# A hybrid encoder layer on one core: x's first two K tiles first, attention's stores by another queue, the last product in two halves

## The chip, the core and the metric

The kernel runs on one core of a Trainium2 chip. The core has a matrix engine (PE, TensorE), three elementwise engines (DVE, the VectorE; ACT, the ScalarE; POOL, the GpSimd) and a queueing engine (SP, the SyncE) that here only starts DMA transfers. ACT and POOL can start transfers too. Each engine runs its own list of instructions in order and waits on semaphores for the others. The metric is the device time of one execution in microseconds, and the median of the runs is what is compared.

## The reference, cut to what matters

x is 1024 tokens by 2048 features in float32. The layer is

```python
def hybrid_layer(x, w_in, w_out, norm_w, decay_fwd, decay_bwd, gn_w, gn_b, sink):
    h = rms_norm(x, norm_w)
    proj = h @ w_in                    # 2048 -> 6656 columns
    rq, rk, rv, rg, aq, ak, av, ag = jnp.split(proj, splits, axis=-1)
    y_ret = retention_branch(rq, rk, rv, decay_fwd, decay_bwd, gn_w, gn_b) * jax.nn.silu(rg)
    y_att = window_attention_branch(aq, ak, av, sink) * jax.nn.silu(ag)
    y = jnp.concatenate([y_ret, y_att], axis=-1)
    return x + y @ w_out               # 2048 -> 2048
```

and a last RMS norm with final_norm_w follows it. Retention has 8 heads of 128 in chunks of 128 tokens, scanned in both directions. The attention has 8 query heads over 2 key and value heads, with a window of 128 tokens on either side and a rotation of the first 32 dimensions.

## The kernel before

**Matmuls.** Every float32 operand is split into a rounded high part and a low part (`split`: a cast on ACT into the high part, then a subtraction on DVE, L84, into the low part), and a product is three matmuls (`mm3`: L98 high by high, L99 and L100 the mixed ones). A matmul of 128x128 by 128x512 is the unit. A K step of an operand pair is 6 of them, and `advance()` is called after each K step of the projection: this is a **tick**. The input projection runs block by block with seven products in place of eight (`PRODUCTS`, in the order 1, 2, 6, 5, 7, 3, 4). Each product has four K steps, that is 24 matmuls. The operands on the side of x are combined once (`put`), kept in DRAM by `keep`, and read back as `c<-kept` by `reload` in the second pass over x's other half of K (`reload` issues one transfer, then idles three ticks). The first block is computed directly (`first_block`), since x isn't yet normalised: the rows of x are scaled by the norm's weights only, and the factor of each token is put in afterwards.

**The start.** Token rows are tiles of 128. Rows 0 to 3 of x come first, as four transfers of one row tile and four K tiles each (128x512). PE transposes them (L1026) into four banks; ACT rounds (`rounded`, L911) and DVE takes the remainder (`left_over`, L915) of each K tile, and `first_block` can start. The 4 x 4 transposes, and turns of the identity that fill the gaps (`turn_ident`), precede the first matmul. Rows 4 to 7 come later. Their squares are summed (`squares`, L371 on ACT, L373 on DVE), the factor is computed (`factors_of`, with a power on POOL, L382), the rows are scaled (`scale_x`), and `rest_of_x` turns them (`turn_x`, L395) one K tile a tick after 15 ticks, with one `split` each.

**The factor of rows 0 to 3** comes later still (`scale_first`, started from `rest_of_x` at its fourth turn): it is spread along a row by a transpose (L960), and DVE multiplies (L965, 12 instructions of 128x512) the eight tiles of `src0` and the four results of the first block that were held unscaled.

**What runs beside the projection.** Generators (`jobs`) are advanced one step a tick: attention, retention and gating each issue a few instructions per tick. The order on PE, SP and POOL is the order of the program text. On ACT and DVE a scheduler orders the instructions from tick 33 to the last product, apart from those that are pinned; before and after that they have the program's order too. Attention first rotates k and q (`rotate`: load `rx` by SP, wait `idle(5)` ticks, then three DVE instructions, L493 and L91, then store). Then `heads(0)`, `(2)`, `(4)` and `(6)` load two query heads each (`q<-pr`), split them (`qbH`, `qbL`), and store their results into `mix` (L602, on SP's queue), 16 stores of 256 KB. A tile of q is overwritten by the head's result, so the next load of q waits for the stores. Results of the projection are stored by SP (the first time) or by POOL's queue with accumulation (L258, the second time).

**The end.** The output projection ends with the product (p, t) = (3, 3). Its bank is added to the residual (`add`, L91), squared and summed (L1305), and `finish` (L1327 to 1337) multiplies by the factor and the weight and stores two halves of 1024 columns of the last row tile. For row tile 6 the same is done by ACT (L1307), POOL (L1310, L1311) and `finish`.

## Time and profile before

| | us |
|---|---|
| median of 3 runs | 1531.56 |
| lowest and highest of them | 1530.33, 1531.64 |
| the profiled execution | 1533.51 |
| its span in the profile | 1531.70 |

The rows shown below are from one profiled execution. Its own time is 1.81 us above its span and 1.95 us above the median. A row of the timeline gives the start in us from the span's beginning, the duration, the engine and line, output and inputs, and how often the instruction is repeated in the row; in brackets stands how long the engine stood idle before it, and what released it. A matmul's duration is longer than the distance to the next one, because matmuls are pipelined: what a step costs is read from start to start. A name with q (SPq, POOLq) means the queueing side of an engine.

### The profile page before, as it was taken

What the parts mean: (1) busy time and instruction counts of PE and PEld (TensorE: products, weight loads), DVE (VectorE), ACT (ScalarE), POOL (GpSimd) and SP (SyncE); (2) the same over time, 40 slices, a digit from 0 to 9 for tenths busy, and PEclk for the clock granted to TensorE, in tenths of its full rate; (3) what the DMA queues carried; (4) which work ended last, traced back from release to release, by engine and by line L of the source; (5) the groups of instructions that cost most, each with busy time, mean ns of one, the idle gap of its engine ahead of it and who ended that gap; (6) DMA issues with size and microseconds to landing.
All of it is one profiled execution on the core that took longest, in us unless ns stands there. A gap on an engine that the chain in (4) does not pass through costs nothing.

```text
span 1531.7 us, 20492 instructions
## 1 busy us (share of the span) xinstructions
PE 1513.6 (99%) x7414; PEld 1273.8 (83%) x7414; DVE 1084.5 (71%) x1940; ACT 690.3 (45%) x1148; POOL 151.8 (10%) x169
## 2 busy tenths in 40 slices
PE   9999999999999999999999999999999999999997
PEld 7788888788888888887888888888888888888886
DVE  6985594557857585746977797779655966776766
ACT  7643363234535453533444434443444643542425
POOL 0000001111010000011212100001111102020001
PEclk9999999999999999999999999999999999999999
DMA  8268656889674415687677655488689769395756
GB/s 302 83 224 297 245 191 167 213 221 253 153 209 135 138 69 179 233 312 203 129 186 197 189 177 193 151 294 295 181 206 256 156 197 265 87 204 163 221 176 254
DMA packets 150533, 306.59 MB, mean 200 GB/s; under 512 B 13440, under 2 KB 71200, under 8 KB 141472
## 3 DMA queue, kind: packets, MB, share of 16 engines
q1 hardware_dynamic: 125632, 250.74, 48.1%
q0 software_dynamic: 19728, 36.71, 15.4%
q10 hardware_dynamic: 5072, 17.84, 3.4%
q8 instruction: 58, 0.95, 0.3%
q14 instruction: 43, 0.35, 0.1%
HBM read 190.68 MB, written 122.95 MB: 205 GB/s over the span
## 4 chain that ended last, share of the span: by engine, by line
PE 78%; issue 13%; DVE 3%; DMA 3%; ACT 1%; POOL 1%; SPq 0%; POOLq 0%; ACTq 0%; DVEq 0%
PE pj L100 19%; PE pj L99 19%; PE pj L98 19%; PE ax L99 5%; PE ax L100 5%; PE ax L98 5%; PE ax L787 2%; PE ax L509 1%; PE ax L586 1%; DMA xt<-in_x_dram 1%; PE ax L754 1%; PE ax L834 1%; DMA c<-kept 1%; DVE c L84 1%; DMA pr<-ct 1%
## 5 line engine op out<-in xcount | busy, mean ns | idle before, releaser
L98 PE MATMUL pj<-c,wH 128*128 128x512 f32 x1448 | 578.6, 400 | 0.3 <-DVE ct L91 0.3
L99 PE MATMUL pj<-c,wH 128*128 128x512 f32 x1448 | 565.3, 390 | 3.2 <-DMA c<-kept 1.7
L100 PE MATMUL pj<-c,wL 128*128 128x512 f32 x1448 | 566.1, 391 | 1.9 <-DVE wL L84 1.9
L100 PEld LDWEIGHTS pj<-c,wL 128*128 128x128 f32 x1448 | 271.8, 188 | 61.8 <-DVE wL L84 4.0
L99 PEld LDWEIGHTS pj<-c,wH 128*128 128x128 f32 x1448 | 272.5, 188 | 54.9 <-DVE c L84 2.2
L98 PEld LDWEIGHTS pj<-c,wH 128*128 128x128 f32 x1448 | 272.3, 188 | 50.4 <-ACT ct L268 0.6
L87 ACT CAST wH<-a 128x1024 fp32r<-128x1024 f32 (+1 forms) x160 | 167.6, 1048 | 248.0 <-PE pj L99 144.9
L84 DVE TENSOR_TENSOR wL<-a,wH 128x1024 fp32r<-128x1024 f32 (+1 forms) x160 | 194.7, 1217 | 112.2 <-ACT wH L87 108.8
L268 ACT COPY ct<-pj 128x512 f32<-128x512 f32 x200 | 116.1, 585 | 234.9 <-PE pj L100 234.3
L91 DVE TENSOR_TENSOR ct<-pj,ct 128x512 f32<-128x512 f32 x170 | 113.2, 689 | 61.4 <-PE pj L100 60.2
L258 POOL DMA_DIRECT2D pr<-ct x104 | 92.3, 962 | 621.9 <-DVE ct L91 474.6
L84 DVE TENSOR_TENSOR wL<-s,wH 128x1024 fp32r<-128x1024 f32 x56 | 68.5, 1223 | 91.7 <-ACT wH L87 91.6
L99 PE MATMUL pj<-wL,c 128*128 128x512 f32 x224 | 87.2, 390 | 0.2 <-DVE wL L84 0.2
L98 PE MATMUL pj<-wH,c 128*128 128x512 f32 x224 | 87.1, 389 | 0.0
L100 PE MATMUL pj<-wH,c 128*128 128x512 f32 x224 | 87.1, 389 | 0.0
L99 PE MATMUL ax<-wL,c 128*128 128x512 f32 x208 | 81.1, 390 | 0.0
L98 PE MATMUL ax<-wH,c 128*128 128x512 f32 x208 | 80.9, 389 | 0.0
L100 PE MATMUL ax<-wH,c 128*128 128x512 f32 x208 | 80.9, 389 | 0.0
L87 ACT CAST wH<-s 128x1024 fp32r<-128x1024 f32 x56 | 59.1, 1056 | 16.4 <-PE ax L100 8.8
L99 PEld LDWEIGHTS pj<-wL,c 128*128 128x128 f32 x224 | 42.0, 188 | 9.4 <-DVE wL L84 0.7
L87 ACT CAST sH<-st 128x128 fp32r<-128x128 f32 x112 | 29.9, 299 | 44.2 <-DVE st L801 28.2
L98 PEld LDWEIGHTS pj<-wH,c 128*128 128x128 f32 x224 | 42.0, 188 | 8.8
(227 smaller groups left out, 2039.9 us busy)
## 6 DMA issues: line engine op xcount, KB each, us to landing
a<-in_w_in_dram SPq DMA_DIRECT2D x103, 512.0 KB, 5.9
kept<-c SPq DMA_DIRECT2D x28, 1024.0 KB, 7.9
c<-kept SPq DMA_DIRECT2D x28, 1024.0 KB, 10.1
pr<-ct SPq DMA_DIRECT2D x104, 256.0 KB, 4.5
pr<-ct POOLq DMA_DIRECT2D x104, 256.0 KB, 6.3
a<-in_w_out_dram SPq DMA_DIRECT2D x18, 512.0 KB, 5.2
rx<-pr SPq DMA_DIRECT2D x64, 128.0 KB, 3.8
ysrc<-mix ACTq DMA_DIRECT2D x16, 512.0 KB, 5.2
```

Source lines behind the costliest of these rows:

```text
L84: nc.vector.tensor_tensor(out=dst, in0=src, in1=high.bitcast(F32), op=ALU.subtract)
L87: nc.scalar.copy(out=dst_h, in_=src)
L91: nc.vector.tensor_tensor(out=dst, in0=a, in1=b, op=ALU.add)
L98: nc.tensor.matmul(po, aH, bH, start=first, stop=False, **kw)
L99: nc.tensor.matmul(po, aH, bL, start=False, stop=False, **kw)
L100: nc.tensor.matmul(po, aL, bH, start=False, stop=last, **kw)
L258: nc.gpsimd.dma_start(out=dst, in_=t, accum_op=ALU.add)
L268: nc.scalar.copy(out=t, in_=bank)
L509: nc.tensor.transpose(pt[:, blk(t)], src[:, blk(b * 4 + t)], ident)
L586: nc.tensor.transpose(pt[:, blk(j)], s[:, blk(j)], ident)
L754: nc.tensor.matmul(sc[:, blk(t)], kT[:, c], qT[:, c], start=True, stop=True)
L787: nc.tensor.matmul(p, k_tok[:, c], vd[:, c, d], start=True, stop=True)
```

## The change

It has six parts.

1. **Start.** The first transfers of x carry two K tiles of two row tiles each, so that K tiles 0 and 1 of all four row tiles arrive first: SP starts row tiles 0 and 1, ACT row tiles 2 and 3. `first_of_first(0)` transposes and splits these two K tiles; the matmuls of the first tick follow, and only then K tiles 2 and 3 (`first_of_first(1)`). The squares of row tiles 0 to 3 move from the start to ticks 11 to 17. The second half of these rows (`xs[5]`, 2 transfers of 1 MB) is loaded at tick 9. `rest_of_x` begins one tick earlier.
2. **Factors of rows 0 to 3.** `scale_first` is started from `sums_of_x` after its last sum. Of the twelve multiplications, four stay on DVE and eight go to POOL (128x512 each).
3. **Rotation.** The first half of the rotation of k waits 8 ticks in place of 5. `put(5)` keeps its place in the order.
4. **Attention's 16 stores into `mix`** go to POOL's queue.
5. **Reload** idles 2 ticks in place of 3.
6. **Last product.** It is computed in two column halves of 256, each followed by its addition, sum of squares and weighting; the final multiplication and the stores are split 768, 512 and 768 columns.

```diff
 def rotate(pool, table, sets, wait):
...
-                yield from idle(5)
+                yield from idle(wait if m == 0 else 5)
...
-                            nc.sync.dma_start(out=mix[RH + i + h][:, half(n // 4)], in_=q[:, h, half(n // 4)])
+                            nc.gpsimd.dma_start(out=mix[RH + i + h][:, half(n // 4)], in_=q[:, h, half(n // 4)])
...
-            yield from rotate_att(att, (T_AK, T_AK + 1))
+            yield from rotate_att(att, (T_AK, T_AK + 1), wait=8)
...
-    load_x(nc.sync, 0)
+    load_first(nc.sync, 0, 0)
     nc.scalar.dma_start(out=vec, in_=norm_w[0].rearrange("(k p) -> k p", p=P))
     half_of_a11(0)
-    load_x(nc.scalar, 1)
-    load_x(nc.sync, 2)
-    load_x(nc.scalar, 3)
+    load_first(nc.scalar, 2, 0)
+    load_first(nc.sync, 0, 1)
+    load_first(nc.scalar, 2, 1)
     half_of_a11(2)
...
+    def first_of_first(c):
+
+        for t in range(4):
+            for k in (2 * c, 2 * c + 1):
+                nc.tensor.transpose(pts[k][:, blk(t)], xh[t, 0][:, blk(k)], ident)
+        if c == 0:
+            prepare()
+        else:
+            split(*(t[:, 2:4] for t in ops_of_a11), a11[:, 2:4])
+        for k in (2 * c, 2 * c + 1):
+            rounded(0, k, pts[k])
+            left_over(0, k, pts[k])
+        for k in (2 * c, 2 * c + 1):
+            keep_bank(0, k, pts[k])
+
     def rest_of_first():
         yield
+        first_of_first(1)
...
 def scale_first():
 
+        yield
+        yield
         factors, rows = ct(), ct()
...
-        for s in range(2):
-            for k in range(M):
-                scale(src0[:, s, k, half(0)])
-                if k % 2:
-                    yield
+        for k in range(M):
+            scale(nc.vector, src0[:, 0, k, half(0)])
+            scale(nc.gpsimd, src0[:, 1, k, half(0)])
+        yield
         yield from idle(31 - clock[0])
         for first, dst, e in unscaled:
-            scale(e)
+            scale(nc.gpsimd, e)
...
-        yield from idle(15)
+        yield from idle(14)
...
-                put(i)
+                put(i, i == 5)
...
-                yield from idle(3)
+                yield from idle(2 if part == 0 else 3)
...
+    def last_half(c, t, bank, rs):
...
+        add(r[:, at], bank, r[:, at])
+        junk = pools["op"].tile([P, HALF], BF16, name="junk", bufs=1)
+        nc.vector.tensor_tensor_reduce(out=junk[:, at], in0=r[:, at], in1=r[:, at], scale=1.0 / D, scalar=rs[c - 1] if c else part[tt],
+                                       op0=ALU.mult, op1=ALU.add, accum_out=rs[c])
+        if c:
+            nc.gpsimd.tensor_tensor(out=rs[1], in0=rs[1], in1=neg_half[:, 0:1], op=ALU.pow)
+        nc.vector.tensor_tensor(out=row[:, to], in0=r[:, at], in1=fw[:, to], op=ALU.mult)
+        if c:
+            lo, hi = 3 * D // 8, 5 * D // 8
+            nc.vector.tensor_scalar(out=row[:, hi:], in0=row[:, hi:], scalar1=rs[1], scalar2=None, op0=ALU.mult)
+            nc.scalar.mul(row[:, :lo], row[:, :lo], rs[1])
+            nc.sync.dma_start(out=out[blk(tt), hi:], in_=row[:, hi:])
+            nc.vector.tensor_scalar(out=row[:, lo:hi], in0=row[:, lo:hi], scalar1=rs[1], scalar2=None, op0=ALU.mult)
+            nc.scalar.dma_start(out=out[blk(tt), :lo], in_=row[:, :lo])
+            nc.sync.dma_start(out=out[blk(tt), lo:hi], in_=row[:, lo:hi])
...
+                            for kk in range(M):
+                                wH, wL = w[p][kk // 2]
+                                mm3(b[:, cols], c[:, 0, kk, blk(t)], c[:, 1, kk, blk(t)], wH[:, kk % 2, cols], wL[:, kk % 2, cols],
+                                    h == 0 and kk == 0, kk == M - 1, skip_group_check=True)
+                            last_half(h, t, b[:, cols], rs)
```

DVE while rows 4 to 7 are turned and the factors of rows 0 to 3 put in. `c` from `src` is the low part of a turned K tile (512 wide) or of `put` (1024 wide), `src<-src,ct` is the factor's multiplication, `wL` the low part of a weight. Before:

```order
L965 TENSOR_TENSOR src<-src,ct 128x512 x2
L84 TENSOR_TENSOR wL<-a_175,wH 128x1024
L84 TENSOR_TENSOR c_512<-src,c_512 128x512
L965 TENSOR_TENSOR src<-src,ct 128x512 x2
L84 TENSOR_TENSOR c_512<-src,c_512 128x512
L965 TENSOR_TENSOR src<-src,ct 128x512 x2
L84 TENSOR_TENSOR c_205<-src,c_205 128x1024
L965 TENSOR_TENSOR src<-src,ct 128x512 x2
L84 TENSOR_TENSOR c_205<-src,c_205 128x1024
```

The same stretch of DVE now, and after it the rows of POOL that hold the moved multiplications:

```order
L84 TENSOR_TENSOR c_492<-src,c_492 128x512 x2
L84 TENSOR_TENSOR wL<-a_175,wH 128x1024
L84 TENSOR_TENSOR c_492<-src,c_492 128x512
L986 TENSOR_TENSOR src<-src,ct 128x512 x4
L84 TENSOR_TENSOR c_203<-src,c_203 128x1024 x2
L84 TENSOR_TENSOR wL<-a_184,wH 128x1024
L84 TENSOR_TENSOR c_204<-src,c_204 128x1024 x2
```

```order
L377 TENSOR_TENSOR rms<-rms,neg_half 128x2 x2
L377 TENSOR_TENSOR rms<-rms,neg_half 128x4
L986 TENSOR_TENSOR src<-src,ct 128x512 x4
L986 TENSOR_TENSOR ct<-ct 128x512 x4
L252 DMA pr_105<-ct 128x512
L252 DMA pr_106<-ct 128x512
```

The multiplications no longer stand between the subtractions of the turned K tiles; four stand behind them on DVE and eight on POOL ahead of its first store.

DVE at the second half of the rotation of k. `rx` is the piece that is rotated, `ct` the result of a product, `wL` the weight of the next one. Before:

```order
L91 TENSOR_TENSOR ct<-pj,ct 128x512 x2
L84 TENSOR_TENSOR wL<-a_2118,wH 128x1024
L493 TENSOR_TENSOR rx_2369<-rx_2369,rt_2365 64x512
L493 TENSOR_TENSOR rx_2370<-rx_2370,rt_2366 64x512
L91 TENSOR_TENSOR ct<-pj,ct 128x512
L91 TENSOR_TENSOR rx_2369<-rx_2369,rx_2370 64x512
L91 TENSOR_TENSOR ct<-pj,ct 128x512
L84 TENSOR_TENSOR wL<-a_2318,wH 128x1024
```

Now:

```order
L91 TENSOR_TENSOR ct<-pj,ct 128x512 x2
L84 TENSOR_TENSOR wL<-a_2110,wH 128x1024
L91 TENSOR_TENSOR ct<-pj,ct 128x512 x2
L84 TENSOR_TENSOR wL<-a_2310,wH 128x1024
L486 TENSOR_TENSOR rx_2382<-rx_2382,rt_2378 64x512
L486 TENSOR_TENSOR rx_2383<-rx_2383,rt_2379 64x512
L91 TENSOR_TENSOR rx_2382<-rx_2382,rx_2383 64x512
```

The product's two additions and the next weight's low part now precede all three instructions of the rotation.

ACT where `heads(2)` loads its queries. `q<-ax` is the last result of the two heads before, `qbH` the high part of the new queries, `wH` that of a weight. Before:

```order
L599 COPY q<-ax 128x2x2x128
L87 CAST wH<-a_3072 128x1024
L87 CAST wH<-a_3581 128x1024
L87 CAST qbH<-q 128x256 x2
L268 COPY ct<-pj 128x512
```

Now:

```order
L592 COPY q<-ax 128x2x2x128
L87 CAST wH<-a_3064 128x1024
L87 CAST qbH<-q 128x256 x2
L87 CAST wH<-a_3573 128x1024
L262 COPY ct<-pj 128x512
```

The cast of a weight now stands behind the two casts that wait for the queries' load.

## Rows read from the trace of the kernel before

**Rows 1.** Page, part 1: busy us, share of the span and instructions of each engine.

```profile
PE 1513.6 (99%) x7414; PEld 1273.8 (83%) x7414; DVE 1084.5 (71%) x1940; ACT 690.3 (45%) x1148; POOL 151.8 (10%) x169
```

**Rows 2.** Timeline of PE: the first matmuls of the first product.

```profile
10.20 0.50 PE L98 MATMUL pj<-c,wH 128*128 128x512 f32 x1
10.98 0.50 PE L99 MATMUL pj<-c,wH 128*128 128x512 f32 x1 [0.28 <-DVE c L915]
```

**Rows 3.** Windows: length; busy PE, PEld, DVE, ACT, POOL; clock, DMA share, GB/s.

```profile
20.00:30.00 10.00, 9.89 (x44) 7.84 (x43) 9.82 (x16) 7.85 (x14) 1.63 (x1) 1.00 1.01 408
...
50.00:60.00 10.00, 8.99 (x40) 6.90 (x39) 10.00 (x13) 7.35 (x10) 0.00 (x0) 1.00 0.17 52
```

**Rows 4.** Timeline of PE: turns of rows 4 to 7 and products, 36 to 78 us.

```profile
36.42 0.50 PE L98 MATMUL pj<-b,wH 128*128 128x512 f32 x1 [0.41 <-ACT b L87]
37.15 0.50 PE L99 MATMUL pj<-b,wH 128*128 128x512 f32 x1 [0.23 <-DVE b L84]
...
52.43 0.39 PE L100 MATMUL pj<-c,wL 128*128 128x512 f32 x1
52.66 0.40 PE L98 MATMUL pj<-c,wH 128*128 128x512 f32 x1
53.20 0.50 PE L99 MATMUL pj<-c,wH 128*128 128x512 f32 x1
...
65.35 0.39 PE L98 MATMUL pj<-c,wH 128*128 128x512 f32 x1
...
76.46 0.39 PE L99 MATMUL pj<-c,wH 128*128 128x512 f32 x1
77.41 0.50 PE L100 MATMUL pj<-c,wL 128*128 128x512 f32 x1 [0.56 <-DVE wL L84]
```

**Rows 5.** Timeline of ACT: the scaling of the last row tile of x.

```profile
31.77 1.16 ACT L387 ACTIVATE xt<-xt,rms 128x1024 f32<-128x1024 f32 x1 [3.37 <-POOL rms L382]
```

**Rows 6.** Lines L965 and L382: ns min/median/max, first and last start, forms.

```profile
L965 DVE TENSOR_TENSOR src<-src,ct x8: 683/691/694, 48.3 to 56.0; 128x512 f32<-128x512 f32 x8
...
L382 POOL TENSOR_TENSOR rms<-rms,neg_half x3: 1012/1143/1629, 26.2 to 41.5; 128x2 f32<-128x2 f32 x2, 128x4 f32<-128x4 f32 x1
```

**Rows 7.** Timeline of DVE and PE at the second half of k's rotation.

```profile
281.20 0.68 DVE L493 TENSOR_TENSOR rx<-rx,rt 64x512 f32<-64x512 f32 x1 [3.52 <-DMA rx<-pr]
...
282.63 0.47 PE L98 MATMUL pj<-c,wH 128*128 128x512 f32 x1 [0.25 <-DVE ct L91]
282.94 0.40 PE L99 MATMUL pj<-c,wH 128*128 128x512 f32 x1
284.27 0.50 PE L100 MATMUL pj<-c,wL 128*128 128x512 f32 x1 [0.93 <-DVE wL L84]
```

**Rows 8.** Timeline of SP and PE at the reload.

```profile
667.95 2.05 SPq L602 DMA_DIRECT2D mix<-q  x2
...
677.34 3.45 SPq L1056 DMA_DIRECT2D c<-kept  x2
...
692.33 0.50 PE L99 MATMUL pj<-c,wH 128*128 128x512 f32 x1 [1.67 <-DMA c<-kept]
```

**Rows 9.** Timeline of SP, ACT and PE where heads(2) loads its queries.

```profile
427.60 0.81 SPq L602 DMA_DIRECT2D mix<-q  x2
...
442.54 0.72 ACT L87 CAST qbH<-q 128x256 fp32r<-128x256 f32 x2 [5.19 <-DMA q<-pr]
...
441.76 0.39 PE L98 MATMUL pj<-c,wH 128*128 128x512 f32 x1
```

**Rows 10.** DMA issues: xcount, KB each, median us from issue to landing.

```profile
pr<-ct POOLq DMA_DIRECT2D x104, 256.0 KB, 6.3
...
q<-pr SPq DMA_DIRECT2D x8, 512.0 KB, 6.3
```

**Rows 11.** Timeline of DVE and SP at the end.

```profile
1522.31 0.75 DVE L1330 SCALAR_TENSOR_TENSOR ra<-r,rs,fw 128x512 f32<-128x512 f32 x1 [1.74 <-POOL rs L1311]
...
1526.80 0.33 SPq L1335 DMA_DIRECT2D out_dram<-ra  x1
```

More of the change, by code (lines that the diff above doesn't have):

```diff
@@ L82, in low, with split @@
     def low(dst, src, high):
-        nc.vector.tensor_tensor(out=dst, in0=src, in1=high.bitcast(F32), op=ALU.subtract)
-    def split(dst_h, dst_l, src):
-        nc.scalar.copy(out=dst_h, in_=src)
-        low(dst_l, src, dst_h)
+        return nc.vector.tensor_tensor(out=dst, in0=src, in1=high.bitcast(F32), op=ALU.subtract)
+    def split(dst_h, dst_l, src, pinned=False):
+        behind(pinned, nc.scalar.copy(out=dst_h, in_=src))
+        behind(pinned, low(dst_l, src, dst_h))
     def add(dst, a, b):
@@ L236, in sums, with put @@
             t.update({5: t1, 6: t2, 4: t2})
-        def put(i):
+        def put(i, pinned=False):
             if i == 7:
@@ L472, in hybrid_layer_kernel, with rotate @@
     load_row(7)
-    for t in (0, 2):
-        load_xs(xs[5][:, t:t + 2], t, 2, slice(PART, D))
-    def rotate(pool, table, sets):
+    def rotate(pool, table, sets, wait):
         for m in range(2):
@@ L499, in rotate, with rotate_att @@
                 yield
-    def rotate_att(pool, *sets):
-        return rotate(pool, rot_a, [([(c, 0, 32) for c in tiles], [(c, r, 16) for c in tiles for r in (16, 0)]) for tiles in sets])
+    def rotate_att(pool, *sets, wait=5):
+        return rotate(pool, rot_a, [([(c, 0, 32) for c in tiles], [(c, r, 16) for c in tiles for r in (16, 0)]) for tiles in sets], wait)
     def transposed(src):
@@ L949, in sums_of_x @@
                 scale_x(t)
+            for t in first.get(n, ()):
+                squares(t, 0, n < 13, 0)
             if n in second:
-                squares(second[n], 1, n < 15)
+                squares(second[n], 1, n == 17)
+                if n == 17:
+                    start(scale_first())
     def scale_first():
+        yield
+        yield
         factors, rows = ct(), ct()
         nc.vector.tensor_copy(out=chunks(factors), in_=rms[:, 0:4].rearrange("p (t o) -> p t o", o=1).broadcast_to([P, 4, P]))
-        yield from idle(2)
+        yield from idle(3)
         pt = ax()
@@ L1303, in summed @@
             rs = op.tile([P, 1], F32, name="rs", bufs=4)
-        if whole and tt == NT - 1:
-            nc.vector.tensor_tensor_reduce(out=junk, in0=r, in1=r, scale=1.0 / D, scalar=part[tt], op0=ALU.mult, op1=ALU.add, accum_out=rs)
-        else:
+        if True:
             nc.scalar.activation(out=junk, in_=r, func=AF.Square, scale=D ** -0.5, accum_out=ssq[:, tt, c:c + 1])
@@ L1391, in hybrid_layer_kernel @@
                 k = 2 * j + q
+                if len(group) == 2 and (p, t) == (3, M - 1):
+                    if k == 0:
+                        sides = [slice(h * 2 * P, (h + 1) * 2 * P) for h in range(2)]
+                        r = rt[3, 1, 2, t]
+                        add(r[:, sides[0]], bank[t][:, sides[0]], r[:, sides[0]])
+                    if k == M - 1:
+                        rs = [pools["op"].tile([P, 1], F32, name="rs", bufs=4) for _ in range(2)]
+                        for h, (b, cols) in enumerate(zip((X[0], bank[t]), sides)):
+                            for kk in range(M):
[3 more added lines that the diff above has]
+                            last_half(h, t, b[:, cols], rs)
+                    at_now[0] += 1
+                    due()
+                    continue
                 mm3(bank[t], c[:, 0, k, blk(t)], c[:, 1, k, blk(t)], wH[:, q], wL[:, q],
```

88 lines of the change are left out of this document (37 added, 51 removed).

## The prediction

> **What bounds the kernel now.** I read the page first, then PE's timeline for places where the distance between two starts is larger than usual, and for each such place the timeline of the engine or queue that ended the wait. PE is busy in 1513.6 of the 1531.70 us of the span [rows 1], so a change that leaves the matmuls alone can give back at most the 18.1 us in which PE stands. A plain matmul starts 0.23 us after the one before it (52.43 to 52.66, [rows 4]); what a start is later than that I call lost.
>
> The losses that this change touches lie in five places. At the start PE has its first product matmul at 10.20 and the second at 10.98, which loses 0.55 [rows 2]. While rows 4 to 7 of x are turned, seven places from 35 to 54 us lose 4.3 us together. Of these [rows 4] shows one near the beginning (36.42 to 37.15, 0.73 less 0.23, so 0.50) and the last (52.66 to 53.20, 0.31). The largest two are 1.1 (a low part on DVE) and 1.0 (the factors' copy on DVE). An eighth loses 0.72 at 76.46 [rows 4]. DVE is busy for all 10.00 of the 10 us from 50 to 60 [rows 3]: it is the late engine there, with ACT behind it. At the rotation of k, a DVE instruction waited out a transfer that ended near 281.9 (DVE had stood 3.52 us by then), and PE lost 0.25 and then 284.27 less 282.94 less 0.23, that is 1.10, on instructions queued behind it [rows 7]; counting the start at 282.63 against the usual distance as well, I get 1.5 in all. At the reload PE waited 1.67 us for `c<-kept`, and lost 1.8 [rows 8]. After PE's end the tail is 9.3 us, and its last issue is at 1526.80 [rows 11].
>
> **The change, part by part.**
>
> *Start.* Half as many bytes of x stand ahead of the first tick, so I expect the first matmul some 1.5 us earlier than 10.20. Little of it lasts. The next K tiles go through the same chain on ACT and DVE: DVE was busy for 9.82 of the 10 us from 20 to 30, and the DMA engines for all of them [rows 3]. Following the chain of casts and low parts by the durations of before, the second operand is there about 0.3 us earlier than it was, and the fifth K tile about 0.25 earlier. So 0.25 us is gained, and 1.5 if the chain were no limit.
>
> *Turns one tick earlier.* The turns need the last row tile of x, which ACT has scaled at 32.93 [rows 5]; that does not come earlier, since it hangs on the loads. PE would arrive about 0.75 us before it: a new loss of 0.75. In return each split has a tick, 1.37 us (six matmuls), more before its product. None of the seven losses is larger than 1.1, so they go if ACT and DVE keep up: 4.3 us. Together with the next part I take off 0.5 for one that stays.
>
> *Factors by POOL.* DVE loses eight multiplications of 0.69 us [rows 6], 5.5 us, in a stretch where it was full, and the four that it keeps come after the last low part of a turned tile. So the loss at 76.46 (0.72), which waits for a weight's low part on DVE, goes as well. What the same multiplication costs on POOL no row shows. POOL's only arithmetic here is a power on 128 x 2 and 128 x 4, at 1.0 to 1.6 us [rows 6], and per column that would be 0.25 us or more, 129 us for 512 columns. The lower end is DVE's own 0.69. The power is another function, and a fixed cost dominates at 4 columns (2 columns cost as much as 4). So I take the value near the multiplication's own row, some 1.2 us, and keep the upper end as a rival. The first four end, by my count, at 47 + 4 x 1.2 = 52, and the operand that needs them is used by the product that starts at 65.35 in the trace of before [rows 4], about 60.9 after the gain of some 4.4 us ahead of it. Between lie a cast of 1.0, a low part of 1.2 and the cast ahead in the queue, 4.2 us in all. So POOL may take until 56.7, or 2.4 us each, before anything is late. The cover is this slack. If it is gone, each 0.1 us of the multiplication costs 0.4. The other four are ahead of POOL's first store, and only stores wait there.
>
> Here the Trainium skill bears on the price. Its page "GPSIMD Engine Reference", section 3.1, gives an addition of two float32 tensors of 2048 elements as 4497 ns on GpSimd against 2293 ns on VectorE; an estimate from this page is 1.1 us for 512. No run here shows it; the sum by it would be the same, since it lies below 2.4.
>
> *Rotation waits 8 ticks.* The transfer that ended at 281.9 is asked for only after two additions and a weight's low part on DVE, as the order shows. Three ticks are 4.1 us, and DVE stood 3.52, so the transfer is there: gain 1.5. What comes later is the rotated k itself, by three ticks; nothing on PE waits for it there, since the loads of k and q follow with waits of their own.
>
> *Stores by POOL, and the reload.* SP's list had `c<-kept` behind two stores of attention that waited for their results until 667.95. So the transfers that were issued from 677.34 came late, and PE waited for the last [rows 8]. Now SP doesn't stand there, and it idles one tick less per transfer. Each of seven pairs is then issued some 2 to 12 us earlier, and the wait of 1.67 is covered: gain 1.8. What is late next is POOL: the retention's table of rotations is queued behind these stores. I get its landing at about 680 and its first use at 687, so no loss.
>
> *Loads of q behind the stores.* Each group of heads loads its queries into the buffer that the stores read. In `heads(2)` the stores were issued at 427.60, and the casts could start at 442.54 [rows 9]. Now two issues on POOL take 1.8 us, a store from POOL's queue lands after 6.3 and the load takes 6.3 (the accumulating stores and the loads of q, [rows 10]): 427.6 + 0.8 + 1.8 + 6.3 + 6.3 = 442.8, as late as before. But now a weight's cast stands behind the casts of the queries on ACT, and its low part on DVE. From the load to that low part is 0.7 + 1.1 + 1.2 = 3.0 us, and the product begins at 441.76 [rows 9]. By the medians PE would lose up to 4.0 us; a plain store should land faster than an accumulating one, and the load is now not behind two other transfers on SP. If it lands at 438.7 or earlier, nothing is lost. I take 0.75 between 0 and 4.0, nearer to the lower end because SP is free. In `heads(4)` and `(6)` the casts had slack of their own, and I take 0.
>
> *Last product.* The halves would help if the addition after PE's end were the next thing. It is not: DVE waits until 1522.31 for POOL's factor of row tile 6 [rows 11], after PE's last matmul has ended, and both halves stand behind that. Before, from there to the last issue were 4.5 us. Now there are six instructions of 256 columns in place of two of 512, each with a fixed part, then a multiplication in three pieces, of which the third waits for the second on DVE. I get the last issue 0.3 to 0.6 later, and a smaller last transfer of 256 KB, which ends some 0.3 sooner after its issue. Sum: 0.2 slower, from -0.3 to +0.7.
>
> **The sum.** Gains: 0.25 + 4.3 + 0.72 - 0.75 - 0.5 = 4.0 ahead of 90 us, 1.5 at the rotation, 1.8 at the reload. Losses: 0.75 at the queries and 0.2 at the end. Net 6.35. The profiled execution of 1533.51 would be 1527.2; the median of the runs, 1531.56, is 1.95 lower, and against it I forecast **1525.2**. The forecast's own range: the head gives 1.5 to 4.8, the queries cost 0 to 3, the tail -0.3 to 0.7. Not all ends together: 1522 to 1528.5.
>
> **Rivals.**
>
> 1. *The start stays bound and the queries are late.* ACT and DVE work through the same casts, plus the squares moved to ticks 11 to 17, and are as late as before; only 1.5 of the head's 4.0 is gained. The queries land by the medians and cost 3. Against it: squares after tick 10 lie behind the last row's scaling, not ahead of it. For it: DVE's 9.82 of 10 [rows 3]. Time: 1531.56 - 1.5 - 1.5 - 1.8 + 3 + 0.2 = 1530.0.
> 2. *POOL's multiplications hold DVE up.* If a DVE instruction with two inputs in SBUF can't run beside one of POOL's, DVE stands for 8 x 1.2 = 9.6 us and is spared 5.5, so it is 4.1 later in a stretch where it is full. The losses at the low parts return (1.1, 0.3 and 0.7, 2.1 us), and as much again may be lost at the following operands. Half of that would leave 6.35 - 3.2, about 1528.4 to 1529.5; I put it at 1529.0. No row of before can speak for or against it, as POOL computes nothing there while DVE is full. Such a rule is stated by the Trainium skill, page "SBUF — State Buffer", section "SBUF: two separate sides": VectorE and GpSimd share one pair of ports, held by one of them for the whole instruction, when the VectorE instruction has two SBUF inputs.
> 3. *POOL is too slow: slower than before.* It decides from the price of one multiplication. Above 2.4 us each the operand is late by 4 x (price - 2.4). The whole gain is used up at 4.0 us, and from 4.8 us the kernel is slower by more than 0.2%. At 6 us each it would be 1525.2 + 14.4 = 1539.6. For it stands only the power's price per column, against it that this price is mostly fixed.
> 4. *The stores don't free anything.* POOL's issues wait for DVE's results like SP's did, the table of rotations and the queries are late, and the reload's 1.8 is lost again, with 1 us beside it. Time: 1528.0. Against it: nothing that PE needs soon was on POOL's queue.
>
> **How the numbers follow.** 0.2% of 1531.56, which is about what a measurement of this kernel can tell from no change, is 3.1 us: faster means below 1528.5, slower above 1534.6. Forecast 0.68, rival 1 0.12, rival 2 0.10, rival 3 0.05, rival 4 0.05. Faster: 0.95 of the forecast's 0.68, a quarter of rival 1, four tenths of rival 2 and most of rival 4, that is 0.65 + 0.03 + 0.04 + 0.04 = 0.76. Slower: rival 3 and a little of rivals 1 and 2, 0.07. The rest, 0.17, is the same. The range that holds the time eight times in ten is the forecast's own range, reaching up over most of rivals 1, 2 and 4: 1521.8 to 1530.2.
>
> **What would show it.** Right: in the profile after, the turns of rows 4 to 7 begin with one wait of under 1 us and run on without those of [rows 4]; no wait of PE near 283 and 690; POOL's multiplications of 1 to 1.5 us. The tail after PE's last matmul is as long as before. Wrong: DVE's instructions beside POOL's multiplications get longer or start later than their inputs (rival 2); POOL's multiplications above 2.4 us (rival 3); a wait of PE near 442 of over 2 us for a weight's low part (rival 1); or new losses at places that the change touches only through the scheduler's order on ACT and DVE, which I have not priced and which would make the prediction wrong without any of its steps being so.

## The result and the profile after

| | before | changed |
|---|---|---|
| median of 6 runs each, side by side | 1531.87 | 1538.50 |
| lowest and highest | 1530.33, 1533.99 | 1535.53, 1540.58 |
| ratio, 95% interval | | 1.0041 [1.003, 1.0052] |
| the profiled execution | 1533.51 | 1539.66 |
| its span | 1531.7 | 1537.9 |

The forecast was 1525.2 with 1521.8 to 1530.2 around it. The kernel became slower by about 6.6 us instead, 0.4%, and the interval of the ratio lies above 1. Part 1 of its page answers to [rows 1]; the group below it is from the page's costliest groups (busy us, mean ns, then PE's idle time just before these matmuls and what ended it).

```profile
PE 1515.0 (99%) x7410; PEld 1275.0 (83%) x7410; DVE 1090.2 (71%) x1938; ACT 688.1 (45%) x1148; POOL 175.7 (11%) x193
...
L100 PE MATMUL pj<-c,wL 128*128 128x512 f32 x1448 | 567.8, 392 | 8.2 <-DVE wL L84 8.1
```

The same group stands on the page of before with this row:

```profile
L100 PE MATMUL pj<-c,wL 128*128 128x512 f32 x1448 | 566.1, 391 | 1.9 <-DVE wL L84 1.9
```

PE waits 6.2 us more for the low parts of weights on DVE. The span is also 6.2 us longer, but that the two are equal is chance: other gains and losses are not in this pair of rows. It tells where to look. The low part is the last link of a weight's chain (load, cast on ACT, subtraction on DVE), so whatever stands ahead of it on DVE and waits, or runs long, ends up here. In the code of the changed kernel L986 is the former L965, L486 the former L493, L734 and L735 the former L741 and L742.

**Where it went.** ACT copies every bank of the projection (`ct<-pj`), so the start of the same copy in two traces shows how far one kernel is behind the other. For example, in the timeline of ACT, before and after:

```profile
127.75 0.59 ACT L268 COPY ct<-pj 128x512 f32<-128x512 f32 x1 [3.42 <-PE pj L100]
```

```profile
129.12 0.59 ACT L262 COPY ct<-pj 128x512 f32<-128x512 f32 x1 [3.42 <-PE pj L100]
```

129.12 less 127.75 is 1.37 us late. Read over all such copies, against the one profiled execution of before, with the kernels of the experiments (negative is ahead):

| stretch of before, us | 15-40 | 95-200 | 300-360 | 452-640 | 700-760 |
|---|---|---|---|---|---|
| changed kernel | -1.2 | +1.4 | +3.1 | +4.4 | +5.2 |
| after_again (the same, later) | +0.5 | +3.0 | +5.4 | +6.1 | +7.0 |
| a_dve_scale | -0.7 | -3.3 | -3.3 | -2.2 | +0.4 |
| a_ct_pool | -0.9 | +0.7 | -0.2 | +2.2 | +5.0 |
| b_pool_scale | 0.0 | +5.7 | +4.6 | +4.6 | +3.9 |
| b_wait8 | -0.1 | -0.1 | -0.3 | -0.3 | -1.9 |
| b_wait9 | -0.8 | -0.8 | -2.8 | -2.8 | -4.0 |
| b_mix | -0.2 | -0.2 | +0.3 | +1.7 | +3.6 |
| b_mix_reload | +0.8 | +0.8 | +0.1 | +1.7 | +3.6 |
| b_mix_pin | -0.6 | -0.7 | -1.4 | +0.5 | +0.2 |
| b_tail | -0.1 | -0.1 | -1.4 | -1.4 | -3.0 |
| best5 | +0.4 | -2.2 | -4.7 | -4.7 | -4.2 |
| best_w9 | -1.3 | -4.0 | -6.4 | -6.4 | -7.4 |

A row's step from one column to the next is what it lost in between. The changed kernel begins 1.2 ahead. Its steps are the head (+2.5 from 40 us on), the rotation (+1.7), the queries (+1.4) and the reload (+0.8); 0.4 more comes before PE's end and 0.5 behind it. Less the 1.2 at the start that is 6.1 of the 6.2 us. Two cautions come from the table itself. The first column differs by 1.6 us between kernels whose start is the same code (b_wait9, b_mix_reload), so the start isn't judged to better than that. With the new start it differs by 1.8; there the granted clock tells part of it, since `after_again` and `best5` have 0.50 from 9 to 11 us, and `best_w9`, `a_ct_pool`, `a_dve_scale` and the changed kernel have 1.00. The steps behind 40 us don't hang on this. And `b_tail`, which changes nothing before 1500 us, gains 1.3 at the rotation and 1.6 at the reload: the profiled execution of before had larger waits there than this one had.

**The head.** PE's timeline in the changed kernel, which answers to [rows 4]: the turns begin with one short stop (30.96 to 31.79 in place of 0.35), no other stop follows up to 54.42 where before had the seven told of with [rows 4], and the product that began at 59.91 in before has its last predecessor at 54.42. Then it stands.

```profile
54.42 0.39 PE L100 MATMUL pj<-b,wL 128*128 128x512 f32 x1
56.19 0.50 PE L98 MATMUL pj<-c,wH 128*128 128x512 f32 x1 [1.39 <-ACT wH L87]
56.53 0.40 PE L99 MATMUL pj<-c,wH 128*128 128x512 f32 x1
60.83 0.80 PE L100 MATMUL pj<-c,wL 128*128 128x512 f32 x1 [3.90 <-DVE wL L84]
61.42 0.63 PE L98 MATMUL pj<-c,wH 128*128 128x512 f32 x1
61.85 0.63 PE L99 MATMUL pj<-c,wH 128*128 128x512 f32 x1
...
64.82 0.39 PE L100 MATMUL pj<-c,wL 128*128 128x512 f32 x1
```

Both waits are for parts of one weight, the high part (`wH`, from ACT) and the low part (`wL`, from DVE). Start to start, 1.54 and 4.07 are lost in them and 0.36 behind them. From 61.42 to 64.82 eight matmuls then take 3.40 us, 0.43 each and not 0.23, another 1.6 us. The windows say why (columns as in [rows 3]): the granted clock falls to the lower of its two levels, 1.2 GHz, while PE stands, and stays there for some 4 us after it.

```profile
58.00:60.00 2.00, 0.00 (x0) 0.00 (x0) 2.00 (x2) 0.98 (x2) 2.00 (x2) 0.50 0.00 0
...
62.00:63.00 1.00, 1.00 (x4) 0.81 (x3) 1.00 (x2) 0.00 (x0) 0.00 (x0) 0.50 0.80 142
...
65.00:66.00 1.00, 1.00 (x6) 0.81 (x6) 1.00 (x2) 0.00 (x0) 0.00 (x0) 1.00 1.05 404
```

DVE and POOL in the same stretch (timeline):

```profile
47.22 6.89 DVE L986 TENSOR_TENSOR src<-src,ct 128x512 f32<-128x512 f32 x4
54.03 4.53 DVE L84 TENSOR_TENSOR c<-src,c 128x1024 fp32r<-128x1024 f32 x2
58.49 2.28 DVE L84 TENSOR_TENSOR wL<-a,wH 128x1024 fp32r<-128x1024 f32 x1
60.69 3.43 DVE L84 TENSOR_TENSOR c<-src,c 128x1024 fp32r<-128x1024 f32 x2
64.05 1.21 DVE L84 TENSOR_TENSOR wL<-a,wH 128x1024 fp32r<-128x1024 f32 x1
```

```profile
47.14 6.42 POOL L986 TENSOR_TENSOR src<-src,ct 128x512 f32<-128x512 f32 x4 [3.88 <-ACT ct L982]
53.53 8.38 POOL L986 TENSOR_TENSOR ct<-ct 128x512 f32<-128x512 f32 x4
```

As long as POOL multiplies, until 61.9, each DVE instruction takes 1.1 us longer: a low part of 1024 columns 2.28 and not 1.21, a multiplication 1.78 and not 0.69 [rows 6]. The weight's low part that PE waits for is one of them. The high part is late for the same reason, since ACT stands for the last of DVE's multiplications just before it casts that weight:

```profile
54.15 1.05 ACT L87 CAST c<-src 128x1024 fp32r<-128x1024 f32 x1 [1.39 <-DVE src L986]
```

**The rotation.** DVE and PE (timelines), which answer to [rows 7], and PE's clock behind it:

```profile
282.64 0.68 DVE L486 TENSOR_TENSOR rx<-rx,rt 64x512 f32<-64x512 f32 x1 [3.92 <-DMA rx<-pr]
```

```profile
284.07 0.47 PE L98 MATMUL pj<-c,wH 128*128 128x512 f32 x1 [0.66 <-DVE ct L91]
...
285.71 0.50 PE L100 MATMUL pj<-c,wL 128*128 128x512 f32 x1 [0.94 <-DVE wL L84]
```

```profile
287.00:289.00 2.00, 2.00 (x7) 1.51 (x6) 1.11 (x1) 0.00 (x0) 0.00 (x0) 0.50 0.66 78
```

The wait of before is still there, with both of its losses, and behind it PE runs at half clock from about 286.7 to 290.1, 1.5 us more.

**The reload.** PE's wait for `c<-kept` [rows 8] is gone. In its place DVE stands 10 us for a small table and PE waits for a weight's low part behind it (DVE, PE):

```profile
685.43 0.29 DVE L734 TENSOR_SCALAR dT<-df,lg 128x128 f32<-128x128 f32 x1 [10.18 <-DMA df<-in_dist_f_dram]
685.63 1.22 DVE L84 TENSOR_TENSOR wL<-a,wH 128x1024 fp32r<-128x1024 f32 x1
```

```profile
684.07 0.39 PE L99 MATMUL pj<-c,wH 128*128 128x512 f32 x1
686.90 0.50 PE L100 MATMUL pj<-c,wL 128*128 128x512 f32 x1 [2.45 <-DVE wL L84]
```

### The profile page after: what moved, and what is told of

Its sections match the earlier page's. It is cut to its first block, busy times and chain, and to the rows that moved or that the text cites. A ratio compares the mean times of both kernels' runs of the same rounds, so it can differ in the third digit from the quotient of the medians.

```text
span 1537.9 us, 20511 instructions
## 1 busy us (share of the span) xinstructions
PE 1515.0 (99%) x7410; PEld 1275.0 (83%) x7410; DVE 1090.2 (71%) x1938; ACT 688.1 (45%) x1148; POOL 175.7 (11%) x193
## 4 chain that ended last, share of the span: by engine, by line
PE 73%; issue 17%; DMA 4%; DVE 3%; POOL 1%; ACT 1%; SPq 0%; POOLq 0%; ACTq 0%; DVEq 0%
PE pj L100 18%; PE pj L98 18%; PE pj L99 18%; PE ax L99 4%; PE ax L100 4%; PE ax L98 4%; PE ax L780 2%; PE ax L502 1%; PE ax L579 1%; DVE wL L84 1%; PE ax L747 1%; PE ax L827 1%; DMA pr<-ct 1%; DMA res<-ct 1%; POOL pr L252 1%
## 5 line engine op out<-in xcount | busy, mean ns | idle before, releaser
L564 DVE CUSTOM_DVE_ANT_0 s<-ax,bnd,snk 128x384 f32<-128x384 f32 (+1 forms) x64 | 34.8, 580 | 21.2 <-PE ax L100 21.0
```

The costliest lines, as they stand in the source:

```text
L564: nc.vector.tensor_tensor_reduce(out=s[:, 0:w], in0=sp[:, 0:w], in1=bnd[:, moff:moff + w], scale=-SCALE, scalar=sink_h, op0=ALU.add, op1=A ...
```

## The experiments

Names with a_ start from the changed kernel, names with b_ from the one before. Ratios are against before, run beside it on the same chip.

**The multiplications on POOL.** `a_dve_scale` takes both edits below, `a_ct_pool` only the first; `b_pool_scale` puts eight on POOL in the old order.

```diff
-            scale(nc.gpsimd, src0[:, 1, k, half(0)])
+            scale(nc.vector, src0[:, 1, k, half(0)])
...
-            scale(nc.gpsimd, e)
+            scale(nc.vector, e)
```

```diff
-                scale(src0[:, s, k, half(0)])
+                scale(nc.gpsimd if s else nc.vector, src0[:, s, k, half(0)])
...
-            scale(e)
+            scale(nc.gpsimd, e)
```

> The changed kernel with the eight multiplications of the factor back on DVE, all else as changed. Theory P (POOL's and DVE's instructions with two inputs in SBUF keep each other out, and PE waits for what DVE could not do): the waits of PE between 54 and 61 us (6.0 us) and the half clock behind them (1.5 us) shrink to 1.5 us or less, DVE's low parts of 1024 columns are back at 1.2 us from 2.3, and the time is 1538.5 - 6 = 1532.5 (1531 to 1534). Rival R (the new order at the start, not POOL, makes DVE late there): the wait for wL stays above 4 us and the time at 1537 to 1539.

Measured: 1534.72, ratio 1.0016 [1.0006, 1.0027], 0.7 above the range expected, with the loss at the reload still in it (2.9, and the half clock behind it). The waits between 54 and 61 us are down to 0.6 and the low parts of 1024 columns back at 1.2, as theory P has it. From 40 us on it is 2.6 us ahead of before where the changed kernel is 2.5 behind: the eight multiplications cost 5.1 us there.

> The kernel before with only the eight multiplications moved to POOL, at their old places. Theory P: the low parts on DVE beside them take about twice as long, and PE loses 3 to 8 us between 48 and 70 us: 1535 to 1540. Rival Q (POOL is only slow by itself, 1.6 us each, and DVE is not touched): the first four end near 55, before DVE ended them in the kernel before (56.7), DVE is 5 us freer, and the time is 1530 to 1532.

Measured: 1537.28, 1.0031 [1.0019, 1.0043], 5.7 us behind at 95 us. This is the run that shows POOL's price by itself, since its first multiplications begin while DVE stands idle. Line L965 (ns min/median/max, first and last start):

```profile
L965 POOL TENSOR_TENSOR src<-src,ct x4: 1265/1284/1730, 45.2 to 48.9; 128x512 f32<-128x512 f32 x4
L965 DVE TENSOR_TENSOR src<-src,ct x4: 678/1758/1768, 49.4 to 58.3; 128x512 f32<-128x512 f32 x4
L965 POOL TENSOR_TENSOR ct<-ct x4: 1708/1718/2243, 50.6 to 56.1; 128x512 f32<-128x512 f32 x4
```

Alone POOL takes 1.27 us and DVE 0.68. Beside each other both take 1.7 to 1.8, and POOL takes 2.24 beside a DVE instruction of 1024 columns: 1.7 to 1.8 is nearly the sum of the two. In the trace their ends alternate, one of POOL, one of DVE, as if each held the other off for one whole instruction. PE pays at a turned K tile's low part, and again at half clock from there (0.79 us for the matmul in place of 0.50):

```profile
56.78 0.79 PE L99 MATMUL pj<-c,wH 128*128 128x512 f32 x1 [5.16 <-DVE c L84]
```

> The changed kernel with only four of the eight multiplications on POOL (the held results of the first block) and the eight of src on DVE. Theory P (each POOL multiplication keeps DVE's two-input instructions out for its 1.3 us): half the dose, DVE is held up by 4 x 1.2 = 5 us less 4 x 0.6 spared, and the time lies between the changed kernel (1538.5) and the one with all on DVE (1534.7), 1535.5 to 1537.5; the DVE instructions beside POOL take 1.7 to 1.8 us at 512 columns. Rival R2 (only the operand that waited for POOL's src results mattered, so that src back on DVE is all): the time is that of the kernel with all on DVE, 1534.7, or below.

Measured: 1537.89, 1.0044 [1.003, 1.0058], 0.4 above the range expected. Half of the multiplications cost nearly as much as all: from 40 us on it is 1.6 us behind, against 2.5 with eight and -2.6 with none, so 4.2 of 5.1. The cost isn't so much for each. By the rows, what counts is how much DVE time stands ahead of the weight's low part, and here DVE has eight multiplications ahead of it. DVE in `a_ct_pool` and in `a_dve_scale`:

```profile
47.45 9.29 DVE L986 TENSOR_TENSOR src<-src,ct 128x512 f32<-128x512 f32 x8
56.66 2.35 DVE L84 TENSOR_TENSOR c<-src,c 128x1024 fp32r<-128x1024 f32 x2
58.93 1.22 DVE L84 TENSOR_TENSOR wL<-a,wH 128x1024 fp32r<-128x1024 f32 x1
```

```profile
47.72 4.90 DVE L986 TENSOR_TENSOR src<-src,ct 128x512 f32<-128x512 f32 x8
52.54 2.35 DVE L84 TENSOR_TENSOR c<-src,c 128x1024 fp32r<-128x1024 f32 x2
54.81 1.22 DVE L84 TENSOR_TENSOR wL<-a,wH 128x1024 fp32r<-128x1024 f32 x1
```

The low part begins at 54.81 with none on POOL, at 58.93 with four and at 58.49 with eight. So in the changed kernel it is 3.7 us later than with all of them on DVE, although four multiplications fewer stand ahead of it there.

**The rotation.** `rotate` with a wait of 8 (`b_wait8`) and of 9 ticks (`b_wait9`) for the first half, in the kernel before; the edit for 9 is shown.

```diff
-                yield from idle(5)
+                yield from idle(wait if m == 0 else 5)
...
-            yield from rotate_att(att, (T_AK, T_AK + 1))
+            yield from rotate_att(att, (T_AK, T_AK + 1), wait=9)
```

> The kernel before with only the longer wait (8 ticks) in the first half of k's rotation. Theory (the wait moves the second half; the DVE instruction that stands for the transfer is the first half's, and the scheduler leaves it ahead of the same two additions): PE's losses near 283 stay, 1531.9 within 1 us. Rival (the forecast's step): the 1.5 us go, 1530.4.

Measured: 1531.75, 0.9998 [0.9988, 1.0007]. DVE waits as before, for the same transfer, and PE behind it:

```profile
280.86 0.68 DVE L493 TENSOR_TENSOR rx<-rx,rt 64x512 f32<-64x512 f32 x1 [4.70 <-DMA rx<-pr]
```

So the prediction's step was wrong, and the order shows how: the instruction that waits belongs to the first half of the rotation. With 8 ticks DVE still has it ahead of the two additions that PE waits for. From the changed kernel:

```
L486 TENSOR_TENSOR rx_2260<-rx_2260,rt_2256 64x512
L91 TENSOR_TENSOR ct<-pj,ct 128x512 x2
L84 TENSOR_TENSOR wL<-a_2006,wH 128x1024
L486 TENSOR_TENSOR rx_2261<-rx_2261,rt_2257 64x512
```

> The kernel before with 9 ticks in the first half of k's rotation. One tick more than in the change, and in the order on DVE the first half's multiplication now stands behind two additions and three weights. Theory: PE's losses near 283 (1.5 us) go, 1530.3 to 1531. Rival (something else holds the additions there): no change, 1532.2.

Measured: 1530.32, 0.999 [0.9981, 0.9999], a gain at the edge of what the medians can tell. One tick more, and the scheduler puts the rotation behind those additions and three low parts:

```
L91 TENSOR_TENSOR ct<-pj,ct 128x512 x2
L84 TENSOR_TENSOR wL<-a_2014,wH 128x1024
L84 TENSOR_TENSOR wL<-a_2052,wH 128x1024
L84 TENSOR_TENSOR wL<-s_2198,wH 128x1024
L493 TENSOR_TENSOR rx_2268<-rx_2268,rt_2264 64x512
```

PE loses nothing there (2.0 us in the table, from -0.8 to -2.8). The six traces whose code is unchanged there lose from 0.7 (`b_tail`) to 1.9 (`b_mix`), the one of before 1.6. DVE's timeline in `b_wait9` has the rotation as a pair without a wait:

```profile
287.69 1.23 DVE L84 TENSOR_TENSOR wL<-s,wH 128x1024 fp32r<-128x1024 f32 x1 [4.21 <-ACT wH L87]
288.83 1.28 DVE L493 TENSOR_TENSOR rx<-rx,rt 64x512 f32<-64x512 f32 x2
```

**The stores on POOL's queue and the reload.**

```diff
-                            nc.sync.dma_start(out=mix[RH + i + h][:, half(n // 4)], in_=q[:, h, half(n // 4)])
+                            nc.gpsimd.dma_start(out=mix[RH + i + h][:, half(n // 4)], in_=q[:, h, half(n // 4)])
...
-                yield from idle(3)
+                yield from idle(2 if part == 0 else 3)
```

> The kernel before with attention's 16 stores on POOL's queue and the reload idling 2 ticks, nothing else. Theory: PE's wait of 1.7 us for c<-kept goes, but retention starts earlier and DVE stands for the distance tables (df, db) with a weight's low part behind it, so PE loses 2 to 3 us near 684; near 442 it loses 1 us for the weight behind the queries' casts: 1533 to 1535 against 1531.9. Rival (the forecast's step): only the 1.8 us are gained and 0.75 lost, 1530.8.

Measured: 1536.28, 1.0026 [1.0016, 1.0037]. That is 1.3 above the range expected. Both losses of the changed kernel are there, 1.6 us at the queries and 1.9 at the reload. I took the shorter reload for the cause of the second.

> The kernel before with the 16 stores on POOL's queue and the reload as it was (3 ticks). Theory: the loss of 2 to 3 us near 680 comes from retention starting earlier through the shorter reload, so it is not there; the wait for c<-kept is gone as SP is free; the queries cost 1.4 near 442: 1531 to 1533. Rival (SP being free is what makes the tables late): the loss near 680 stays, 1535.5 to 1536.5 as with both.

Measured: 1537.3, 1.0035 [1.0023, 1.0048], with the stores alone. The loss at the reload is the same, so that theory fell. DVE in `b_mix`:

```profile
682.19 0.29 DVE L741 TENSOR_SCALAR dT<-df,lg 128x128 f32<-128x128 f32 x1 [9.70 <-DMA df<-in_dist_f_dram]
682.39 1.22 DVE L84 TENSOR_TENSOR wL<-a,wH 128x1024 fp32r<-128x1024 f32 x1
```

And in before:

```profile
675.04 1.23 DVE L84 TENSOR_TENSOR wL<-a,wH 128x1024 fp32r<-128x1024 f32 x1 [4.24 <-ACT wH L87]
680.93 0.29 DVE L741 TENSOR_SCALAR dT<-df,lg 128x128 f32<-128x128 f32 x1 [4.67 <-DMA df<-in_dist_f_dram]
```

The table `df` lands at about the same time, 680.9 and 682.2. Only the order of two neighbours on DVE has changed: in before the weight's low part stood ahead of `dT`, now it stands behind it. The edit doesn't mention either; the scheduler came out so.

> The kernel before with the 16 stores on POOL's queue, as in the run of that part alone, and the first head's decay (dT) kept in program order, which puts it behind three weights' low parts on DVE in place of ahead of one. Theory (PE's loss near 681 is a low part queued behind the instruction that waits for the distance tables): that loss of 2.1 us and the half clock behind it go, the loss near 442 stays: 1533 to 1535 against 1537.3. Rival (the stores on POOL's queue make retention late in another way): 1536.5 or more.

The edit pins the first head's `dT` behind three low parts:

```diff
-                nc.vector.tensor_scalar(out=dT, in0=df, scalar1=lg[:, h:h + 1], scalar2=None, op0=ALU.mult)
+                behind(h == 0, nc.vector.tensor_scalar(out=dT, in0=df, scalar1=lg[:, h:h + 1], scalar2=None, op0=ALU.mult))
```

Measured: 1535.02, 1.0018 [1.0008, 1.0027]. The loss behind the stop at 682 is gone, which settles its cause. But the old wait is back (PE, then SP):

```profile
692.54 0.50 PE L99 MATMUL pj<-c,wH 128*128 128x512 f32 x1 [1.36 <-DMA c<-kept]
```

```profile
676.81 0.95 SPq L170 DMA_DIRECT2D a<-in_w_in_dram  x2
677.85 2.86 SPq L1056 DMA_DIRECT2D c<-kept  x2
```

None of attention's stores stands on SP here, and the pair that PE waits for is still issued at 677.85, against 677.34 in [rows 8]: ahead of it are two loads of weights, begun at 676.81. So the stores weren't what held it back. The shorter reload does move it: with it SP has issued its last `c<-kept` of this stretch by 655.6 in `b_mix_reload` and by 658.3 in the changed kernel, ahead of those loads, while `b_mix` has it at 684.67. The shorter reload without the stores was not run.

**The last product.** `b_tail` has part 6 of the change alone, with the edit shown in the diff of the change.

> The kernel before with only the last product by half the columns. Theory (DVE still waits for row tile 6's factor first, and the chain behind it has more instructions): the span ends 9.6 to 9.8 us after PE's last matmul in place of 9.3, the time is 0.2 to 0.6 us longer, 1532.5. Rival (the halves help as meant): 1 us shorter, 1531.

Measured: 1532.56, 1.0001 [0.9992, 1.001]. From PE's last matmul to the span's end it has 9.8 us, before had 9.2: its cost is below what the medians can tell.

**The whole again, and two combinations.** `after_again` is the changed kernel once more. `best5` has the new start with all multiplications on DVE, the rotation's wait of 9, the stores on POOL's queue for the last two heads only, `dT` pinned, and the old reload and last product. `best_w9` is the changed kernel with these edits, and the old last product:

```diff
-            scale(nc.gpsimd, src0[:, 1, k, half(0)])
+            scale(nc.vector, src0[:, 1, k, half(0)])
...
-            scale(nc.gpsimd, e)
+            scale(nc.vector, e)
...
-            yield from rotate_att(att, (T_AK, T_AK + 1), wait=8)
+            yield from rotate_att(att, (T_AK, T_AK + 1), wait=9)
...
-                            nc.gpsimd.dma_start(out=mix[RH + i + h][:, half(n // 4)], in_=q[:, h, half(n // 4)])
+                            nc.sync.dma_start(out=mix[RH + i + h][:, half(n // 4)], in_=q[:, h, half(n // 4)])
...
-                yield from idle(2 if part == 0 else 3)
+                yield from idle(3)
```

> The changed kernel once more, for a second profile. If the half clock behind the loss near 283 (1.5 us) belongs to this stall by chance of its moment, it can be absent here, with PE 1.7 us better off there; the loss near 57 and the half clock behind it (7.5 us together) are there again. Time 1537 to 1539.

Measured: 1540.29, 1.0048 [1.0033, 1.0063], 1.3 above the range expected; every loss named above is in its trace again, the half clock behind the rotation too.

> A combination: the changed kernel's start with all multiplications on DVE, 9 ticks in k's rotation, stores on POOL's queue for the last two query heads alone, the first head's decay kept in program order, reload at 3 ticks and the last product as before. From the parts: start -3.3, rotation -1.5 to -2, wait for c<-kept 0 to -1.7, nothing lost at the queries: 1532.3 - 5.8 = 1526.5 (1525 to 1528.5). Rival (the parts meet, and what is gained early is waited for at the reload's transfers): 1529 to 1531.

Measured: 1528.8, 0.9979 [0.997, 0.9988], 0.3 above the range expected and 0.2 below the rival's. It loses nothing at the queries, and waits 2.15 us for `c<-kept` at the reload.

> The same without stores on POOL's queue and without the pinned decay: start with all multiplications on DVE and 9 ticks in the rotation alone. 1532.3 - 3.3 - 1.7 = 1527.3 (1526 to 1529); against the combination it shows whether moving the last stores is worth anything.

Measured: 1527.02, 0.9966 [0.9953, 0.9978]: 5.3 us faster than before, and 11.5 and 13.3 below the two medians of the changed kernel. It keeps the two parts of the change that pay, the start and the rotation, the second with 9 ticks in place of 8.

## Why the prediction was wrong

**Head: the gain was there, and POOL took it.** The forecast had 4.0 for the start, the turns and the stop at 76.46. Without POOL's multiplications the three kernels with the new start are ahead by 2.6 from 40 us on (a_dve_scale, best5, best_w9), and by -0.4 to 1.3 from the start itself. The stop forecast for the first turn, 0.75, was 0.48, and the seven losses of the turns are gone. The mechanism was right, and the size, 2.2 to 4.0 with the start, is within its range of 1.5 to 4.8. Against the gain stand three new stops of PE in all three traces, of 0.5 to 1.0 for weights' low parts on DVE, 2.2 together between 55 and 76 us.

**The step that failed is "Factors by POOL".** Its price of 1.2 us was right, 1.27 measured. But the step compared that price with the slack of POOL's own results (2.4 us each), and counted DVE as relieved by 5.5 us. POOL's results were in time: beside DVE they took 1.6 each, and the first four ended at 53.56, ahead of the 56.7 that the step allowed. (Its terms for that bound, 1.0, 1.2 and a cast, give some 3.2 and not 4.2; nothing hangs on it.) DVE was not relieved, it was held: each of POOL's multiplications cost the DVE instruction beside it 1.1. This is rival 2, whose working had DVE 4.1 late; by the rows the weight's low part comes 3.7 to 4.2 late (11.3 us from the first multiplication to it, 47.22 to 58.49, against 7.1, 47.72 to 54.81). By the rule of the Trainium skill that was named there ("SBUF — State Buffer", section "SBUF: two separate sides"), one engine holds the shared ports for a whole instruction; the alternation in the rows agrees. Rival 2 then failed in its last step: it spread the delay over several small stops and took half. In the rows all of it lies ahead of one weight, PE loses 5.6 us waiting for its two parts, and 1.6 more at half clock after. The cost is 5.1 and not 3.2, and rival 2 had too small a chance.

The prediction says that no row of before can speak for or against it. That is a misreading: POOL's power on 128x2 and 128x4 isn't its only arithmetic there. Eight powers on 128x8 each start beside a DVE instruction that reads two operands from SBUF, and such rows speak for rival 2. Two of them, before (POOL, then the DVE instruction beside each):

```profile
757.07 2.50 POOL L855 TENSOR_TENSOR rstd<-rstd,neg_half 128x8 f32<-128x8 f32 x1 [11.09 <-DVE rstd L854]
1108.76 2.23 POOL L855 TENSOR_TENSOR rstd<-rstd,neg_half 128x8 f32<-128x8 f32 x1 [8.93 <-DVE rstd L854]
```

```profile
756.81 1.23 DVE L91 TENSOR_TENSOR a<-a,a 128x1024 f32<-128x1024 f32 x1
1108.24 1.23 DVE L84 TENSOR_TENSOR wL<-s,wH 128x1024 fp32r<-128x1024 f32 x1
```

The same power takes 2.50 and 2.23 us, but ends 1.53 and 1.52 after DVE's instruction does. Over all eight it ends 1.50 to 1.53 after the last such instruction, also where DVE's next ones read a bank (`ct<-pj,ct`). So POOL stood for DVE. That DVE would stand for POOL, the half that costs PE its time, these rows don't show: DVE's instructions beside the power last as long as elsewhere.

**Rotation: a gain of 1.5 forecast, a loss of 1.7 measured.** The step "Rotation waits 8 ticks" failed. The prediction showed the order of the rotation's second half and took it for the instruction that had waited. The one that waits is the first half's, and 8 ticks leave it where it was. The remedy was one tick short (`b_wait9`: 2.0, of which part is the large wait in the one execution of before that was profiled). The additional loss is the half clock after it; it came in both traces of the changed kernel and in no other one, though `b_wait8` has the same two waits of PE. Why it falls there is open.

**Stores and reload: a gain of 1.8 forecast, a loss of 0.8 measured.** The wait for `c<-kept` did go, as forecast, but the step "Stores by POOL, and the reload" had three things wrong. SP's stores were not what made it late (`b_mix_pin`); the shorter reload moves the issue. A price of 1.8 from one execution was too much, as PE loses only 0.2 to 1.1 there in `b_tail`, `b_wait8`, `b_wait9` and `b_pool_scale`, whose code is the same in that place. What sets the landing of that transfer from run to run wasn't settled. And the new loss of 2.6 is the kind that the prediction named and did not price: the order of two DVE instructions that the change never mentions. It could have been read beforehand, from the order of both kernels around every load that lands late.

**Queries: mechanism right, a loss of 1.4 in place of 0.75.** The casts of the queries start at 443.53 and the weight's cast behind them; PE loses 0.40 and 0.70 and a little more. Against [rows 9], ACT in the changed kernel:

```profile
443.53 0.71 ACT L87 CAST qbH<-q 128x256 fp32r<-128x256 f32 x2 [8.54 <-DMA q<-pr]
444.15 1.05 ACT L87 CAST wH<-a 128x1024 fp32r<-128x1024 f32 x1
```

The changed kernel is 3.1 us late when it comes here, so the load landed at 440.4 on the clock of the prediction, between its bound of 438.7 and its estimate by the medians, 442.8. By its own count that costs 1.7. One reason may be that these stores land after 3.6 us (median), where the count had the 6.3 of the accumulating ones. The value taken, 0.75, lay near the lower end of what came: `after_again` loses 0.7 there, and the other traces with all the stores on POOL's queue 1.1 to 2.4.

**Last product: right.** The wait for POOL's factor, 1522.31 in [rows 11], stands now at 1527.77, and the last issue of SP at 1532.95. From PE's last matmul to that issue's end are 5.1 us against 4.6 (DVE, then SP). The forecast of 0.3 to 0.6 for the issue holds; the 0.3 that the smaller transfer should have given back did not come. In the trace of before PE's last matmul ends at 1522.51, 0.2 after that wait and not ahead of it as the prediction has it; both halves stand behind the wait all the same.

```profile
1527.77 0.75 DVE L1355 SCALAR_TENSOR_TENSOR ra<-r,rs,fw 128x512 f32<-128x512 f32 x1 [1.40 <-POOL rs L1312]
```

```profile
1532.95 0.37 SPq L1350 DMA_DIRECT2D out_dram<-ra  x1
```

In sum: of the terms, the head moved from -4.0 to +1.4 with its start, the rotation from -1.5 to +1.7, the reload from -1.8 to +0.8, the queries from +0.75 to +1.4 and the end from +0.2 to +0.5; 0.4 between the reload and the end was in no term. The turns, the queries and the tail came as their steps describe them; the steps that trusted another engine to take over work, or a wait to be where it wasn't, did not.

## What to carry to other kernels

Work moved from DVE to POOL doesn't relieve DVE while both read two operands from SBUF: count each such POOL instruction as time taken from DVE (here 1.1 us for each multiplication that takes 1.27 alone), and look at what stands behind on DVE. When a scheduler sets an order, compare the two orders around every instruction that waits long for a transfer, whether or not the change mentions it, and identify the waiting instruction by the number of its tile and not by its line. And take the price of a wait on a transfer from several executions, since one may hold it at its largest (here 1.8, and 0.2 in another).

## What was not expected of the hardware

- POOL and DVE alternate by whole instructions: 512 columns take 1.27 us on POOL and 0.68 on DVE alone, 1.73 and 1.77 together; 1024 columns on DVE go from 1.21 to 2.28, and POOL's 512 beside them from 1.27 to 2.25. POOL's small powers are held too: on 128x8 they end 1.50 to 1.53 us after DVE's instruction with two operands in SBUF, however long that still runs.
- A wait of PE can cost more than itself. Behind 5.6 us of waits, broken by two matmuls, the granted clock was 0.50 for some 4 us of work, 1.6 us lost; in the changed kernel it was also 0.50 from 287 to 289 after waits of 0.66 and 0.94 only, where `b_wait8` with the same waits lost nothing more. Behind a wait of 1.96 it fell to 0.51 in `b_mix`, and behind the 2.45 of the changed kernel's reload it didn't.
- Two loads of small tables (`df` and `db`, 128x128 each) took 9.7 and 9.3 us from issue to landing, with the DMA engines at 0.80 to 1.09 from 676 to 684 us; in the chain of waits of the changed kernel that is the piece that ended last there:

```profile
676.26 9.32 DMA db<-in_dist_b_dram
```
